# First mixer: normalising the window attention's probabilities in the product that turns them

## The chip, the cores and the metric

The kernel runs on one core of a Trainium2 chip. The metric is the device time of one execution in microseconds; the time before is the median of three runs. The engines are called as in the profile: PE (matrix products), PEld (the loading of PE's stationary operand, beside PE), DVE (elementwise work and reductions), ACT (activation functions and copies), POOL (small elementwise work, some DMAs) and SP (most DMAs).

## The reference, cut to what matters

The program is an encoder trunk of two layers. Layer 0 has windowed attention as its token mixer, layer 1 a gated linear recurrence; each mixer also has four cross-attention heads into 256 memory tokens, and each layer ends with a convolutional feed-forward part. There are 1024 tokens of width 1024, all in fp32. The change lies in the windowed attention of layer 0, with 16 query heads and 4 key heads of width 64:

```python
def window_gqa_sink(q, k, v, sink):
    ...
    s = jnp.einsum('bnqhgd,bnkhd->bnhgqk', qb, kb, preferred_element_type=F32) * (d ** -0.5)
    ...
    s = jnp.where(valid[None, :, None, None], s, -jnp.inf)
    sk = sink.astype(F32).reshape(hkv, grp)[None, None, :, :, None, None]
    m = jnp.maximum(jnp.max(s, axis=-1, keepdims=True), sk)
    p = jnp.exp(s - m)
    p = p / (jnp.sum(p, axis=-1, keepdims=True) + jnp.exp(sk - m))
    o = jnp.einsum('bnhgqk,bnkhd->bnqhgd', p.astype(v.dtype), vb)
```

A block of 128 queries sees its own 128 keys and the 128 on each side. The row sum by which `p` is divided includes the sink's term.

## The kernel before, in words

The attention is in `window()`. It works on four head groups `g` (one key head and four query heads each), and for each of them on eight blocks `n` of 128 queries: 32 blocks of four heads. `proj(g)` makes a group's queries, keys and values out of the normed input (tile `pj`, three products for each pair of operands, L84 to L86, where each operand is split into a high and a low part), applies the rotation and turns the result by transposes (tile `ptq`, L320). `attend(g, ...)` does the blocks.

In a block, for each of the four heads `j`: two products give the scores in `ps` (L366, L367; two banks), and one DVE instruction adds the mask and writes the negated scores to `sm` with their minimum in `nm` (L369). ACT then makes the exponentials in place and their sums `su` (L373); the sink stands as one more column behind the scores, put there by POOL (L362). `rd` is the reciprocal of the four sums (L375). Then the rows of `sm` are scaled by `rd`, head 0 on ACT (L378), heads 1 to 3 on DVE (L380). For each of the two or three key blocks `c`, four PE transposes (L385, one for each head, `sm` as the stationary operand and the identity `ident` as the moving one) put the turned probabilities into a bank `pt` (two banks), and ACT, or DVE for `c == 1`, copies it to `pT` (L387). The products with the values `v` into `po` follow at L395, in plain fp32, with high priority. There are 22 key blocks in eight query blocks, so 88 in all and 352 transposes.

The memory cross-attention (`cross_unit`) runs between the blocks with banks of the same names. The kernel already has a product with a diagonal, at its start (L1509 to L1513): the rows' scale `rsm` times the identity is `dg`, and `ones` times `dg` spreads it over the partitions, in fp32.

What order the instructions have on an engine is settled when the kernel is built: a scheduler runs a timeline model of the whole program and issues by priorities, so a change of one step moves others around it. Within an engine instructions run in that order. While a group's blocks run, the projection of the next group is spread between them; beside the last group stands the output projection (`pb`, class `Out`).

Of the kernel before, what the change touches and what calls it, by code (L numbers as in the profile page):

```python
# [8 lines left out]
F32 = mybir.dt.float32  # L9
# [3 lines left out]
AF = mybir.ActivationFunctionType  # L13
# [5 lines left out]
P = 128  # L19
# [30 lines left out]
def build(tc, A, out):  # L50
    nc = tc.nc
    act, dve, pool, pe = nc.scalar, nc.vector, nc.gpsimd, nc.tensor
# [13 lines left out]
    ident = cp.tile([P, P], F32, name="ident")  # L66
# [21 lines left out]
    def split(h, l, src):  # L88
        return act.copy(h, src), dve.tensor_tensor(l, src, h.bitcast(F32), op=ALU.subtract)  # L89
# [103 lines left out]
    def cross_head(l, h, wp, behind=None):  # L193
        kvh = wp.tile([P, 2, 256], F32R, tag="kvh", bufs=1, name="kvh")
        kvl = wp.tile([P, 2, 256], F32R, tag="kvl", bufs=1, name="kvl")
        raw = kvl.bitcast(F32)
        nc.sync.dma_start(raw, kvd[l][h])
        with tc.issue_after(behind.ins) if behind else nullcontext():
            act.copy(kvh, raw)
        dve.tensor_tensor(kvl, raw, kvh.bitcast(F32), op=ALU.subtract)  # L200
        return *wunit(A["wxq"][l, h]), kvh, kvl
# [47 lines left out]
    def window():  # L249
        ea = tc.alloc_tile_pool(name="attn0", bufs=1, reuse_waits="tile")  # L250
        ap_ = tc.alloc_tile_pool(name="attn", bufs=2, side="right", reuse_waits="tile")
# [25 lines left out]
        def proj(g):  # L277
# [56 lines left out]
            if g == 0:  # L334
                rqs = [token(t) for t in range(5)]
                turn(0, rqs[:4])
                attend(0, kept, range(3))
                turn(1, rqs[4:] + [token(t) for t in range(5, NT)])
            else:
                for b in range(2):  # L340
                    turn(b, [token(t) for t in range(4 * b, 4 * b + 4)])
# [6 lines left out]
        def attend(g, qkv, blocks=range(NT)):  # L348
            qs, kh, kl, v = qkv
            for b in range(2):  # L350
                for nn in range(4):
                    n = 4 * b + nn
                    if n not in blocks:
                        continue
                    if nn % 2 == 0 and g < 3:
                        pairs[0] = [ea.tile([P, 2, 256], F32R, tag=x, bufs=2, name=x) for x in ("oh", "ol")]
                    lo, hi = max(n - 1, 0), min(n + 2, NT)
                    w = (hi - lo) * P
                    mo = (lo - (n - 1)) * P
                    sm = ap_.tile([P, 4, 385], F32, tag="sm", bufs=3, name="sm")  # L360
                    st = {x: ap_.tile([P, 4], F32, tag=x, name=x) for x in ("nm", "su", "rd")}
                    pool.tensor_copy(sm[:, :, w:w + 1], sk[:, 4 * g:4 * g + 4].unsqueeze(2))  # L362
                    for j in range(4):
                        s = psp.tile([P, 384], F32, tag="ps", bufs=2, name="ps")
                        m = slice(nn * P, (nn + 1) * P)
                        pe.matmul(s[:, :w], qs[j][b][:, m], kh[:, lo * P:hi * P], start=True, stop=False)  # L366
                        pe.matmul(s[:, :w], qs[j][b][:, m], kl[:, lo * P:hi * P], start=False, stop=True)  # L367
                        hd = 4 * g + j
                        dve.tensor_tensor_reduce(out=sm[:, j, :w], in0=s[:, :w], in1=wmask[:, mo:mo + w],  # L369
                                                 scale=-0.125, scalar=sk[:, hd:hd + 1], op0=ALU.add, op1=ALU.min,  # L370
                                                 accum_out=st["nm"][:, j:j + 1])
                    for j in range(4):
                        marks[g, n] = act.activation(sm[:, j, :w + 1], sm[:, j, :w + 1], AF.Exp, bias=st["nm"][:, j:j + 1],  # L373
                                                     scale=-1.0, accum_out=st["su"][:, j:j + 1])
                    dve.reciprocal(st["rd"], st["su"])  # L375
                    for j in range(4):
                        if j < 1:
                            act.activation(sm[:, j, :w], sm[:, j, :w], AF.Copy, scale=st["rd"][:, j:j + 1])  # L378
                        else:
                            dve.tensor_scalar_mul(sm[:, j, :w], sm[:, j, :w], st["rd"][:, j:j + 1])  # L380
                    pTs = []
                    for c in range(hi - lo):
                        tp = psp.tile([P, 4, P], F32, tag="pt", bufs=2, name="pt")
                        for j in range(4):
                            pe.transpose(tp[:, j, :], sm[:, j, c * P:(c + 1) * P], ident)  # L385
                        pT = ap_.tile([P, 4, P], F32, tag="pT", bufs=3, name="pT")
                        (dve.tensor_copy if c == 1 else act.copy)(pT, tp)  # L387
                        pTs.append(pT)
                    po = psp.tile([P, 2, P], F32, tag="po", bufs=1, name="po")
                    with tc.high_priority(AHEAD):  # L390
                        mm = None
                        for c in reversed(range(hi - lo)):
                            for i in range(2):
                                with tc.issue_after(mm.ins) if mm else nullcontext():
                                    mm = pe.matmul(po[64 * i:64 * i + 64], v[:, lo + c, :], pTs[c][:, i::2, :],  # L395
                                                   start=c == hi - lo - 1, stop=c == 0, tile_position=(0, 64 * i))
                    if g == 3:
                        split(uh[:, 6:8, n * P:(n + 1) * P], ul[:, 6:8, n * P:(n + 1) * P], po)
                        continue
                    split(*(x[:, :, (nn % 2) * P:(nn % 2 + 1) * P] for x in pairs[0]), po)  # L400
                    if nn % 2 == 1:
                        ts_ = slice((n - 1) * P, (n + 1) * P)
                        for i, x in enumerate(pairs[0]):
                            nc.sync.dma_start(oS[2 * g:2 * g + 2, :, i, ts_].rearrange("a p t -> p a t"), x.bitcast(F32))
                if 4 * b + 3 not in blocks:
                    continue
                for _ in range(XU[g][b]):
                    xh_, xb_ = units.pop(0)
                    if xb_ == 0:
                        xhead[0] = cross_head(0, xh_, ea, None if xh_ else marks[0, 3])  # L410
                    cross_unit(0, xh_, xb_, xhead[0], ap_, tags, ea, pair)
# [3 lines left out]
        for g in range(3):  # L415
            attend(g, cur, range(0 if g else 3, NT))
            cur = proj(g + 1)
        ea.release()
        tables.release()
        attend(3, cur)  # L420
        wo0.open()
        y0 = wo0.w1.tile([P, NT, 512], F32, bufs=1, name="y0")
# [1207 lines left out]
```

## Time and profile before

| what | value |
| --- | --- |
| median of 3 runs | 2615.66 us (2615.55 to 2616.15) |
| profiled execution, its own time | 2614.47 us |
| span of its instructions | 2612.7 us, 39059 instructions |
| PE busy / its weight loads | 2587.9 us (99%) / 2172.6 us (83%) |
| DVE / ACT / POOL busy | 1762.1 us / 1332.8 us / 453.5 us |
| TensorE clock granted in the span | 1.00 |
| transposes of L385 | first start 98.8 us, last 460.1 us |

A group's row has the line of the program, the engine, the operation, the tiles (written<-read), the shape, how many, then the busy time in us with the mean of one in ns, and the idle time of the engine ahead of them with what ended it. In a timeline row the first two numbers are start and length in us; a merged row (x8) runs from the first start to the last end. A matmul's record overlaps the next one's, so PE's busy share alone doesn't say how full it is.

### The profile page before, as it was taken

Reading aid. Unit: us, or ns where it says so; the run is one execution under the profiler, and the core shown is the slowest. Engines: PE = TensorE matmul, PEld = TensorE weight load, DVE = VectorE, ACT = ScalarE, POOL = GpSimd, SP = SyncE. Lnnn points to the kernel's source line nnn. Section 1 sums busy time; section 2 is a strip of 40 time slices with the busy share of each in tenths; the row PEclk is TensorE's granted clock in tenths of the full one; section 3 lists DMA queues with packets and bytes.
Section 4 is the critical chain, followed back from the end, with each engine's and each line's share of the span. In section 5 each row is a group of like instructions: output and inputs, shape, how many; then the busy total and the mean of one; then the engine's idle time right before and its main releaser. Section 6 shows DMA issues by size and latency. Waiting matters only on the chain.

```text
span 2612.7 us, 39059 instructions
## 1 busy us (share of the span) xinstructions
PE 2587.9 (99%) x14596; PEld 2172.6 (83%) x14596; DVE 1762.1 (67%) x2839; ACT 1332.8 (51%) x2395; POOL 453.5 (17%) x520
## 2 busy tenths in 40 slices
PE   8999999999999999999999999999999999999998
PEld 8988887888888888887888888888888888888887
DVE  6677775577565664488698696987768655656447
ACT  6566665444444454454555454555534444444453
POOL 0431110211111100032133131221211111110013
PEclk9999999999999999999999999999999999999999
DMA  9782342467877757673236341213337777875666
GB/s 357 257 204 67 101 147 60 141 179 201 209 209 201 190 160 262 194 266 109 80 130 167 81 113 41 61 38 109 130 113 189 212 202 195 206 204 175 211 192 237
DMA packets 203918, 431.17 MB, mean 165 GB/s; under 512 B 20048, under 2 KB 64464, under 8 KB 198096
## 3 DMA queue, kind: packets, MB, share of 16 engines
q1 hardware_dynamic: 169744, 329.30, 38.7%
q0 software_dynamic: 24544, 90.19, 16.5%
q10 hardware_dynamic: 9440, 9.19, 1.1%
q8 instruction: 114, 1.87, 0.3%
q14 instruction: 76, 0.62, 0.1%
HBM read 333.18 MB, written 119.54 MB: 173 GB/s over the span
## 4 chain that ended last, share of the span: by engine, by line
PE 91%; DVE 5%; DMA 2%; ACT 1%; issue 0%; POOL 0%; SPq 0%; ACTq 0%; DVEq 0%; POOLq 0%
PE X L580 31%; PE V L580 11%; PE pj L84 7%; PE pj L85 7%; PE pj L86 7%; PE Y L580 5%; PE pb L84 4%; PE pb L85 4%; PE pb L86 4%; PE po L395 2%; PE pt L385 1%; PE po L1344 1%; PE pa L1265 1%; PE pu L1320 1%; PE ps L366 1%; PE pt L122 1%
## 5 line engine op out<-in xcount | busy, mean ns | idle before, releaser
L89 DVE TENSOR_TENSOR wl<-st,wh 128x1024 fp32r<-128x1024 f32 (+1 forms) x238 | 261.6, 1108 | 315.3 <-ACT wh L89 282.7
L89 ACT CAST wh<-st 128x1024 fp32r<-128x1024 f32 (+1 forms) x238 | 221.6, 937 | 268.0 <-PE X L580 172.2
L580 PE MATMUL X<-wh,wl 128*128 128x512 f32 x528 | 204.8, 389 | 0.0
L580 PE MATMUL X<-wl,wh 128*128 128x512 f32 x528 | 204.8, 389 | 0.0
L84 PE MATMUL pj<-uh,wh 128*128 128x512 f32 x512 | 202.3, 396 | 2.4 <-DVE s L1187 1.4
L86 PE MATMUL pj<-uh,wl 128*128 128x512 f32 x512 | 202.1, 395 | 0.0
L85 PE MATMUL pj<-ul,wh 128*128 128x512 f32 x512 | 201.5, 394 | 0.1
L580 PE MATMUL X<-wh 128*128 128x512 f32 x528 | 198.0, 390 | 0.1
L84 PE MATMUL pj<-wh,uh 128*128 128x384 f32 (+1 forms) x512 | 189.1, 370 | 2.0 <-DVE gs L1168 1.4
L85 PE MATMUL pj<-wl,uh 128*128 128x384 f32 (+1 forms) x512 | 187.1, 365 | 0.0
L86 PE MATMUL pj<-wh,ul 128*128 128x384 f32 (+1 forms) x512 | 186.9, 365 | 0.0
L80 DVE TENSOR_TENSOR wl<-st,wh 128x1024 fp32r<-128x1024 f32 (+1 forms) x91 | 118.3, 1306 | 29.3 <-ACT wh L79 28.1
L580 PE MATMUL V<-uh,wh 128*128 128x512 f32 x336 | 130.7, 389 | 0.0
L580 PE MATMUL V<-ul,wh 128*128 128x512 f32 x336 | 130.7, 389 | 0.0
L580 PE MATMUL V<-uh,wl 128*128 128x512 f32 x336 | 130.7, 389 | 0.0
L580 PEld LDWEIGHTS X<-wh 128*128 128x128 f32 x528 | 99.1, 188 | 21.1 <-issue 0.5
L79 ACT CAST wh<-st 128x1024 fp32r<-128x1024 f32 (+1 forms) x97 | 97.5, 1014 | 37.0 <-PE pj L85 23.9
L580 PEld LDWEIGHTS X<-wl,wh 128*128 128x128 f32 x528 | 99.1, 188 | 20.7 <-DVE wl L89 0.2
L580 PEld LDWEIGHTS X<-wh,wl 128*128 128x128 f32 x528 | 99.1, 188 | 20.4
L84 PEld LDWEIGHTS pj<-uh,wh 128*128 128x128 f32 x512 | 96.3, 188 | 21.9 <-DVE q L1182 1.4
L85 PEld LDWEIGHTS pj<-ul,wh 128*128 128x128 f32 x512 | 96.3, 188 | 19.2 <-DVE ul L89 0.4
L86 PEld LDWEIGHTS pj<-uh,wl 128*128 128x128 f32 x512 | 96.3, 188 | 18.9 <-issue 0.4
(412 smaller groups left out, 6986.7 us busy)
## 6 DMA issues: line engine op xcount, KB each, us to landing
st<-hid SPq DMA_DIRECT2D x154, 256.0 KB, 3.1
st<-in_ffw_dram SPq DMA_DIRECT2D x108, 256.0 KB, 3.3
w2s<-in_ffw_dram POOLq DMA_DIRECT2D x24, 1024.0 KB, 8.4
st<-in_ffw_dram SPq DMA_DIRECT2D x46, 512.0 KB, 4.3
hid<-tt SPq DMA_DIRECT2D x88, 256.0 KB, 4.8
st<-w2s SPq DMA_DIRECT2D x88, 256.0 KB, 3.3
sx<-in_ffw_dram SPq DMA_DIRECT2D x84, 256.0 KB, 3.9
sy<-in_ffw_dram SPq DMA_DIRECT2D x42, 512.0 KB, 6.4
```

The lines of the kernel that those rows point to most:

```text
L79: act.copy(h[:, :n], raw)
L80: (eng or dve).tensor_tensor(l[:, :n], raw, h[:, :n].bitcast(F32), op=ALU.subtract)
L84: pe.matmul(o, ah, bh, start=first, stop=False)
L85: pe.matmul(o, ah, bl, start=False, stop=False)
L86: return pe.matmul(o, al, bh, start=False, stop=last)
L89: return act.copy(h, src), dve.tensor_tensor(l, src, h.bitcast(F32), op=ALU.subtract)
L122: across = pe.transpose(ps[:, k, :], u[:, (4 * b + k) * P:(4 * b + k + 1) * P], ident)
L366: pe.matmul(s[:, :w], qs[j][b][:, m], kh[:, lo * P:hi * P], start=True, stop=False)
L385: pe.transpose(tp[:, j, :], sm[:, j, c * P:(c + 1) * P], ident)
L395: mm = pe.matmul(po[64 * i:64 * i + 64], v[:, lo + c, :], pTs[c][:, i::2, :], start=c == hi - lo - 1, stop=c == 0, tile_position=(0, 64 * i))
L580: last = pe.matmul(o, x, y, start=new, stop=e, skip_group_check=not first)
L1265: return pe.matmul(pa[i:i + 32, c, j:j + n], x[:, c * P + i:c * P + i + 32], y[:, c * P + j:c * P + j + n], start=True, stop=True, tile_po ...
```

## The change

The scaling at L378 and L380 goes. Instead DVE multiplies the identity by each head's `rd` (a diagonal of 128 x 128 for each head, in a new tile `dg` with two buffers), and the transpose by the identity becomes a plain fp32 product with that diagonal: out[k, q] = sum over r of sm[r, k] * dg[r, q], which is the turned and scaled block. ACT's part of the scaling has no successor.

```diff
                     dve.reciprocal(st["rd"], st["su"])
+                    dg = ap_.tile([P, 4, P], F32, tag="dg", bufs=2, name="dg")
                     for j in range(4):
-                        if j < 1:
-                            act.activation(sm[:, j, :w], sm[:, j, :w], AF.Copy, scale=st["rd"][:, j:j + 1])
-                        else:
-                            dve.tensor_scalar_mul(sm[:, j, :w], sm[:, j, :w], st["rd"][:, j:j + 1])
+                        dve.tensor_scalar_mul(dg[:, j, :], ident, st["rd"][:, j:j + 1])
                     pTs = []
                     for c in range(hi - lo):
                         tp = psp.tile([P, 4, P], F32, tag="pt", bufs=2, name="pt")
                         for j in range(4):
-                            pe.transpose(tp[:, j, :], sm[:, j, c * P:(c + 1) * P], ident)
+                            pe.matmul(tp[:, j, :], sm[:, j, c * P:(c + 1) * P], dg[:, j, :], start=True, stop=True)
```

In the changed kernel the lines behind this place have numbers lower by two: the products stand at L383, the copies at L385, `v*pT` at L393.

The scheduler lays the attention's instructions out anew. The first place is PE's order in the first block of the first group. Before:

```order
L84 MATMUL pj<-uh,wh 128x512
L385 MATMUL pt<-ident,sm 128x128 x2
L366 MATMUL ps<-kh,qs 128x384
L385 MATMUL pt<-ident,sm 128x128 x6
L367 MATMUL ps<-kl,qs 128x384
L85 MATMUL pj<-ul,wh 128x512
```

and now:

```order
L84 MATMUL pj<-uh,wh 128x512
L366 MATMUL ps<-kh,qs 128x384
L367 MATMUL ps<-kl,qs 128x384
L85 MATMUL pj<-ul,wh 128x512
L383 MATMUL pt<-dg,sm 128x128 x8
L366 MATMUL ps<-kh,qs 128x384
```

The block's eight products stand in one row, behind a head's scores and one projection product that stood within or behind the transposes.

The second place is PE's order at the start of the last head group, where no projection product stands between (`ptq` are the turned queries and keys, `po` the products with the values). Before:

```order
L320 MATMUL ptq<-ident,rq 128x128 x4
L366 MATMUL ps<-kh,qs 128x384
L367 MATMUL ps<-kl,qs 128x384
L385 MATMUL pt<-ident,sm 128x128 x8
L366 MATMUL ps<-kh,qs 128x384
L367 MATMUL ps<-kl,qs 128x384
L366 MATMUL ps<-kh,qs 128x384
L367 MATMUL ps<-kl,qs 128x384
L395 MATMUL po<-pT,v 64x256 x4
```

Now, from the third of six heads whose scores stand in a row:

```order
L366 MATMUL ps<-kh,qs 128x384
L367 MATMUL ps<-kl,qs 128x384
L366 MATMUL ps<-kh,qs 128x384
L367 MATMUL ps<-kl,qs 128x384
L366 MATMUL ps<-kh,qs 128x384
L367 MATMUL ps<-kl,qs 128x384
L366 MATMUL ps<-kh,qs 128x384
L367 MATMUL ps<-kl,qs 128x384
L383 MATMUL pt<-dg,sm 128x128 x8
L320 MATMUL ptq<-ident,rq 128x128 x4
```

The scores of six heads now come ahead of the block's products with the diagonal, where one to two heads stood between the other products.

The third place is DVE's order in the first block (`L369 ISA` is the masked minimum; each has a second instruction that reads out its result). Before:

```order
L380 TENSOR_SCALAR sm<-sm,rd 128x256 x3
L300 TENSOR_TENSOR t_1203<-pj,sin 128x320
L80 TENSOR_TENSOR wl<-st,wh 128x768
L369 ISA sm,nm<-ps,wmask,sk 128x384
L369 ISA nm 128x1
L387 COPY pT<-pt 128x512
```

and now:

```order
L378 TENSOR_SCALAR dg<-ident,rd 128x128 x4
L300 TENSOR_TENSOR t_1206<-pj,sin 128x320
L80 TENSOR_TENSOR wl<-st,wh 128x768
L369 ISA sm,nm<-ps,wmask,sk 128x384
L369 ISA nm 128x1
L369 ISA sm,nm<-ps,wmask,sk 128x384
L369 ISA nm 128x1
L385 COPY pT<-pt 128x512
```

Four diagonals stand where the three scalings stood, and the copy of the turned bank comes one head's minimum later. Behind the last block, in the output projection, PE's order is again what it was, from its 2330th row on.

## The prediction

> **What bounds the kernel now.** I read the page first, for the engine that sets the time.
>
> ```profile
> PE 2587.9 (99%) x14596; PEld 2172.6 (83%) x14596; DVE 1762.1 (67%) x2839; ACT 1332.8 (51%) x2395; POOL 453.5 (17%) x520
> ...
> PE 91%; DVE 5%; DMA 2%; ACT 1%; issue 0%; POOL 0%; SPq 0%; ACTq 0%; DVEq 0%; POOLq 0%
> ```
>
> PE is busy all the time, and 91% of the chain that ends last is PE's; the next engine, DVE, is busy for two thirds. But a busy PE need not be a full one: a matmul's record lasts longer than the time after which the next one may start. So I looked next at the timeline, for the distance from one start to the next, which is the price of an instruction on PE. These are, in order of time, the two products with a diagonal that the kernel already has at its start, six transposes of the changed line, eight transposes of a later norm, and four records of a plain fp32 product in the second mixer with what follows them (columns: start and length of the group in us, engine, line, out<-in, shape, count).
>
> ```profile
> 19.22 0.61 PE L1513 MATMUL pbc<-dg,ones 128*128 128x128 f32 x4
> ...
> 99.20 0.82 PE L385 MATMUL pt<-ident,sm 128*128 128x128 f32 x6
> ...
> 505.30 1.03 PE L122 MATMUL pt<-ident,nu 128*128 128x128 f32 x8
> ...
> 1313.46 0.61 PE L1344 MATMUL po<-S,qin 128*128 128x128 f32 x4
> 1313.91 0.39 PE L1344 MATMUL po<-v,As 128*128 128x128 f32 x2
> ```
>
> A merged row runs from the first start to the last end, and one record is 0.275 us long (the mean in the groups below). Eight transposes: (1.03 - 0.275) / 7 = 0.108 us from start to start; six: (0.82 - 0.275) / 5 = 0.109. I take **0.109 us for a transpose**. Four records of L1344: (0.61 - 0.275) / 3 = 0.112 us, and the starts agree, since 1313.46 to 1313.91 is 0.45 for four. L1513: 0.112 again. For the `v*pT` products there is a row of the chain of waits, which gives a record 1.45 / 12 = 0.121 us:
>
> ```profile
> 213.74 1.45 PE po L395 x12
> ```
>
> Is the attention stretch, where the change is, really full of such starts? I counted one window of it by the groups of instructions, kept apart by shape.
>
> ```profile
> L86 PE MATMUL pj<-wh,ul 128*128 128x384 f32 x38 | 12.8, 338 | 0.0
> L84 PE MATMUL pj<-wh,uh 128*128 128x384 f32 x37 | 12.8, 345 | 0.0
> L85 PE MATMUL pj<-wl,uh 128*128 128x384 f32 x37 | 12.5, 338 | 0.0
> L385 PE MATMUL pt<-ident,sm 128*128 128x128 f32 x52 | 7.6, 275 | 0.0
> L395 PE MATMUL po<-pT,v 128*64 128x256 f32 x60 | 7.6, 388 | 0.1
> L366 PE MATMUL ps<-kh,qs 128*128 128x384 f32 x18 | 6.7, 374 | 0.0
> L367 PE MATMUL ps<-kl,qs 128*128 128x384 f32 x18 | 6.1, 337 | 0.0
> ```
>
> This is 200 to 240 us. The 148 records of 384 columns at 0.174 us (the first two starts in the dense stretch below are 0.17 apart; 0.174 is the median of all such distances) are 25.8, 52 transposes at 0.109 are 5.7, 60 records of L395 at 0.121 are 7.3; with 4 transposes and 2 short score products not shown, some 0.7, that is 39.5 of 40 us. So PE has under 2% to spare here: **what is added to PE's own work in this stretch is added to the time**, and what is taken from ACT and DVE is not.
>
> **The change part by part.** The groups of the touched lines in the window 60 to 480 us:
>
> ```profile
> L385 PE MATMUL pt<-ident,sm 128*128 128x128 f32 x352 | 50.5, 275 | 0.6 <-ACT sm L378 0.6
> ...
> L380 DVE TENSOR_SCALAR sm<-sm,rd 128x384 f32<-128x384 f32 (+1 forms) x96 | 33.4, 406 | 0.8
> ...
> L378 ACT ACTIVATE sm<-sm,rd 128x384 f32<-128x384 f32 (+1 forms) x32 | 18.9, 590 | 3.4 <-DVE rd L375 3.3
> ```
>
> *PE.* The 352 transposes have one record each and become 352 products of an fp32 tile of 128 x 128 with an fp32 diagonal. What such a product is made of, the answer on the tile `dg` at the kernel's start tells:
>
> ```profile
> L1513 PE MATMUL pbc<-dg,ones x4: 273/274/275, 19.2 to 19.6; 128*128 128x128 f32 x4
> L1512 DVE TENSOR_SCALAR dg<-ident,rsm x2: 280/284/288, 16.7 to 16.9; 128x128 f32<-128x128 f32 x2
> ```
>
> There the program has two products (the loop over t at L1511 runs twice) and the trace four records, so a product is two passes. At 0.112 us each that is 0.224 per product against 0.109 per transpose: **+0.115 us x 352 = +40.5 us**, on PE and with nothing on PE to hide it. The ends of this term are 0.114 and 0.117 per product by the rounding of the rows, 40.1 and 41.2 us. Which operand is held in the array does not change: `sm` was loaded before and is now.
>
> [...]
>
> *ACT.* It loses 18.9 us of scaling. *DVE* loses 33.4 us and gets 128 rows of `dg` (four in each of 32 blocks) of 128 x 128, at 0.284 by L1512: 36.4 us, so +3.0. Both lie beside PE's matmuls, and I cost them at nothing; without that cover DVE's 3.0 us would be its price, and ACT's 18.9 us its gain. The way of one block stays as long: from `rd` to the last scaled head three times 0.406 us on DVE, now four times 0.284; 1.22 against 1.14 us.
>
> *Waits that can go.* PE's own waits in 60 to 500 us, the four longest of six rows:
>
> ```profile
> PE po L395 <- ACT pT L387: 0.9, 2, 0.7
> PE pt L385 <- ACT sm L378: 0.6, 1, 0.6
> PE po L395 <- DVE pT L387: 0.6, 1, 0.6
> PE pb L84 <- ACT y L492: 0.6, 1, 0.6
> ```
>
> These are 2.7 us in five waits, 3.4 with the two rows left out. A wait shows only beyond the end of the record before it, so each hides up to 0.17 us more (a 384-column record is 0.34 long, and the next may start after 0.17): 3.4 + 7 x 0.16 = 4.5 us is the most that can come back. One of them is of the removed step; the place is the start of the last head group, where there is little projection work between the score products:
>
> ```profile
> 385.06 0.34 PE L366 MATMUL ps<-kh,qs 128*128 128x384 f32 x1
> 385.23 0.34 PE L367 MATMUL ps<-kl,qs 128*128 128x384 f32 x1
> 386.15 1.08 PE L395 MATMUL po<-pT,v 128*64 128x256 f32 x8 [0.58 <-DVE pT L387]
> ...
> 389.49 0.34 PE L367 MATMUL ps<-kl,qs 128*128 128x384 f32 x1
> 390.42 1.09 PE L385 MATMUL pt<-ident,sm 128*128 128x128 f32 x8 [0.59 <-ACT sm L378]
> ...
> 391.89 0.34 PE L367 MATMUL ps<-kl,qs 128*128 128x384 f32 x1
> 392.78 0.50 PE L84 MATMUL pb<-wh,uh 128*128 128x512 f32 x1 [0.56 <-ACT y L492]
> ```
>
> From start to start, less 0.174 each, 0.75 + 0.76 + 0.72 = 2.2 us are lost here. The middle one waits for ACT's scaled head and goes: **-0.8**. DVE's diagonals are then what is late next.
>
> *Waits that can come.* At the same place the new order has six heads' score products in a row with nothing between (second place in the section on the change). There are two score banks, and DVE empties one in 0.612 us (the median, in the answer on the tile `sm`):
>
> ```profile
> L369 DVE CUSTOM_DVE_ANT_0 sm<-ps,wmask,sk x128: 474/612/621, 86.0 to 446.5; 128x384 f32<-128x384 f32 x96, 128x256 f32<-128x256 f32 x32
> ```
>
> PE needs 2 x 0.174 = 0.35 for a head, so from the third of the six on it waits 0.26 for each: 4 x 0.26 = **+1.1 us**. Behind the waiting score product stand, in order, the products with the diagonal, then the transposes of queries. Bounds: nothing, if DVE is ahead; and if three more stretches of the new order (one per head group) lose as much as this one did, 3 x 2.2 = 6.6 us more.
>
> Sum, on the profiled execution's 2614.47 us (span 2612.7): + 40.5 - 0.8 + 1.1 = 2655.3. The median of the three runs is 1.2 us above that execution, so **2656.5 us**.
>
> **The rivals.**
>
> *A transpose costs as much as its record is long, and the products are cheaper (faster).* The place is PE at L385, the price 0.275 us for each of 352 transposes against 0.224 now: 352 x 0.051 = -18.0 us, 2597.7 us. It decides if eight transposes in a row take more than 1.8 us. For it speaks only the mean of 275 ns; against it the eight in 1.03 us. [...]
>
> *PE has hidden room.* The products fill gaps that the page calls busy. 0.5 us in 40 were not accounted for above; over the 410 us of attention that is 5, with the dense stretch's 2.2 some 7. Even if all of it took up passes, 2649 us. To come out not slower, 40 us would be needed.
>
> [...]
>
> *The product is done as a transpose is, in one pass.* Then the change does not do what it says: 352 x (0.112 - 0.109) = +1.1 us, 2616.8. Against it, L1513 again, whose moving operand is a diagonal too.
>
> *Waits of a new kind in every block.* If each of the 32 blocks lost one wait like those in the dense stretch, 0.75 us, it would be 24 us more, 2680. For it: PE's order is rearranged from the first block to the output projection behind the last, and DVE has 3 us more to do. Against it: a bank of products now takes PE 0.90 us where four transposes took 0.44, so those who empty it (ACT's copies) have twice the time.
>
> **How the numbers follow.** The forecast has 0.89. Its range: below, 2615.7 + 40.1 - 4.5 = 2651; above, 2615.7 + 41.2 + 1.1 + 6.6 = 2664.6. I set 2650 to 2665; the room of the second rival reaches to its lower end. The others: faster 0.01, hidden room that takes more than 7 us 0.03, four passes 0.02, one pass 0.01, waits in every block 0.04. A measurement of this kernel tells a difference from none at about 0.2%, 5 us. So faster by more 0.01, within it 0.02 (the one pass, and a hundredth for room that I don't see), slower 0.97.
>
> **What would show it.** The line of the products should have 704 records in place of 352, with eight of them (four products) from start to start in 0.9 us. L378's group is gone from ACT, `dg` stands on DVE with 128 rows of about 0.28 us. From 500 us on, everything stands as before and some 41 us later. I am wrong in the price if the records are 352 or 1408, wrong in the cover if the span grows by over 50 us with 704 records at 0.112, and wrong on the room if it grows by under 34.

## The result, and the profile after

The changed kernel takes **2659.5 us** (median of four runs, 2658.56 to 2662.13) beside 2615.61 us for the one before on the same chip: ratio 1.0169, interval 1.0157 to 1.0181, so 43.9 us slower. The forecast was 2656.5 us in a range of 2650 to 2665. The profiled execution is the highest of the four, 2662.13 us with a span of 2660.4, which is 47.7 us more than the span before. So readings of this trace hold for 47.7 us, and the medians for 43.9. One execution each of e4, e6 and e12 below ran for 3235 to 6689 us and is left out of their medians, ranges and ratios.

The page of the kernel after, first busy time by engine, then the share of each engine in the chain that ended last:

```profile
PE 2631.3 (99%) x14948; PEld 2217.7 (83%) x14948; DVE 1760.2 (66%) x2871; ACT 1318.0 (50%) x2363; POOL 447.6 (17%) x520
...
PE 86%; DVE 7%; DMA 3%; ACT 1%; issue 1%; POOL 1%; SPq 0%; ACTq 0%; DVEq 0%; POOLq 0%
```

PE has 352 records more, and ACT and DVE are a little less busy than before. PE has lost five points of the chain, two of them to DVE: somewhere PE stands and waits. Both parts show in closer views. First the groups of the touched lines in the window 60 to 540 us:

```profile
L383 PE MATMUL pt<-dg,sm 128*128 128x128 f32 x704 | 92.3, 278 | 0.0
...
L378 DVE TENSOR_SCALAR dg<-ident,rd 128x128 f32<-128x128 f32 x128 | 31.1, 305 | 0.9
```

704 records stand where 352 stood, none of them after a wait. The distance from start to start is in PE's timeline, in the first block:

```profile
100.08 1.95 PE L383 MATMUL pt<-dg,sm 128*128 128x128 f32 x16
```

Eight products are 16 records, and (1.95 - 0.275) / 15 = 0.112 us. The price of one product is 0.224 us, as forecast.

The waits are in PE's own list for 60 to 540 us (waiting tile and line, what for, us in all, times, longest):

```profile
PE pb L84 <- ACT v L304: 2.5, 1, 2.5
PE ps L366 <- ACT kh L89: 1.3, 1, 1.3
PE ps L366 <- DVE nm L369: 1.1, 2, 0.8
```

The two longest are neighbours. This is PE's timeline at that place, the start of the last head group:

```profile
401.77 0.60 PE L320 MATMUL ptq<-ident,rq 128*128 128x128 f32 x4
403.68 0.50 PE L366 MATMUL ps<-kh,qs 128*128 128x256 f32 x2 [1.31 <-ACT kh L89]
406.68 0.80 PE L84 MATMUL pb<-wh,uh 128*128 128x512 f32 x1 [2.50 <-ACT v L304]
407.27 0.63 PE L85 MATMUL pb<-wl,uh 128*128 128x512 f32 x1
407.69 0.63 PE L86 MATMUL pb<-wh,ul 128*128 128x512 f32 x1
...
412.73 0.40 PE L86 MATMUL pb<-wh,ul 128*128 128x512 f32 x1
```

From start to start, less 0.109 for each transpose and 0.120 for each product of 256 columns, PE loses 1.91 - 0.44 = 1.5 us and then 3.00 - 0.24 = 2.8 us. After that the records are 0.63 us long where 0.39 is usual, and their starts are 0.42 to 0.43 us apart where they are 0.227 apart elsewhere: 14 starts take 412.73 - 406.68 = 6.05 us and would take 3.18, another **2.9 us**. The view by windows has the reason (PE, PEld, DVE, ACT and POOL busy with their counts, then PE's granted clock, the DMA share and GB/s):

```profile
400.00:406.00 6.00, 2.87 (x18) 2.39 (x16) 5.97 (x6) 3.60 (x4) 2.15 (x2) 0.98 0.81 227
406.00:413.00 7.00, 6.33 (x16) 4.98 (x17) 1.76 (x4) 0.63 (x2) 2.29 (x4) 0.53 0.61 240
413.00:426.00 13.00, 11.86 (x69) 9.51 (x68) 8.25 (x30) 6.70 (x20) 0.14 (x1) 1.00 0.01 1
```

The granted clock falls to a half during the second wait (0.89 over 405 to 406 us, 0.50 over 406 to 407), and in the 6 us of the first window DVE is busy for 5.97 and PE for 2.87. What PE waits for is in the timelines of ACT and of DVE:

```profile
398.84 4.17 ACT L79 CAST wh<-st 128x1024 fp32r<-128x1024 f32 x4 [0.69 <-PE pj L86]
403.04 0.59 ACT L89 CAST kh<-ptq 128x512 fp32r<-128x512 f32 x1
```

```profile
399.93 5.42 DVE L80 TENSOR_TENSOR wl<-st,wh 128x1024 fp32r<-128x1024 f32 x4 [1.05 <-ACT wh L79]
405.39 0.49 DVE L299 TENSOR_TENSOR t<-pj,cos 128x320 f32<-128x320 f32 x1
405.79 0.48 DVE L300 TENSOR_TENSOR t<-pj,sin 128x320 f32<-128x320 f32 x1
```

Four weight tiles of the output projection are cast on ACT and split on DVE; behind them in the queues stand the keys `kh` and the last rotations of this group's projection. Only after these rotations does ACT get to `v` (L304), the instruction that the profile names as the one PE waits for: the output projection (`pb`) is written into the banks of `pj`, which the rotations and `v` still read. PE has nothing to put in: in its order no projection product stands between the group's last one and the output projection.

### The profile page after: what moved, and what is told of

Same layout as the page of the kernel before. It is cut to its first block, busy times and chain, and to the rows that moved or that the text cites. A ratio compares the mean times of both kernels' runs of the same rounds, so it can differ in the third digit from the quotient of the medians.

```text
span 2660.4 us, 39787 instructions
## 1 busy us (share of the span) xinstructions
PE 2631.3 (99%) x14948; PEld 2217.7 (83%) x14948; DVE 1760.2 (66%) x2871; ACT 1318.0 (50%) x2363; POOL 447.6 (17%) x520
## 4 chain that ended last, share of the span: by engine, by line
PE 86%; DVE 7%; DMA 3%; ACT 1%; issue 1%; POOL 1%; SPq 0%; ACTq 0%; DVEq 0%; POOLq 0%
PE X L578 27%; PE V L578 11%; PE pj L84 7%; PE pj L85 7%; PE pj L86 7%; PE Y L578 4%; PE pb L84 4%; PE pb L85 4%; PE pb L86 4%; PE pt L383 3%; PE po L393 2%; PE po L1342 1%; DVE wl L89 1%; PE pa L1263 1%; PE pu L1318 1%
## 5 line engine op out<-in xcount | busy, mean ns | idle before, releaser
L373 ACT ACTIVATE sm<-sm,nm 128x385 f32<-128x385 f32 (+1 forms) x128 | 75.1, 587 | 75.2 <-DVE nm L369 71.3
```

## Experiments

Two questions are open: is the price that of the second pass, with the softmax side worth nothing; and does the hole at 402 to 413 us (PE's two long waits and the half clock with them) belong to the diagonals or to the order the scheduler happened to make? To count, I took the starts of PE and subtracted from each distance the price of the instruction by its width (0.227 us for 512 columns, 0.174 for 384, 0.120 for 256, 0.109 for a transpose, 0.112 for a pass of the product, 0.121 for `v*pT`). A pass, here as in the prediction, is one record of a product. What is left over is time in which PE is late. The table has this for one profiled execution of each kernel, worked out by me from the trace; the third row is the first three head groups, the fourth from 6 us ahead of the first `pb` product to 30 us behind it.

| us | before | after | e1 | e9 | e2 | e6 |
| --- | --- | --- | --- | --- | --- | --- |
| span | 2612.7 | 2660.4 | 2652.1 | 2654.4 | 2622.5 | 2621.8 |
| sum of prices | 2579.4 | 2619.9 | 2619.9 | 2619.9 | 2579.4 | 2579.4 |
| late, three groups | 8.6 | 6.8 | 6.5 | 6.7 | 15.7 | 12.6 |
| late, start of last group | 3.3 | 9.8 | 3.0 | 2.6 | 3.6 | 7.2 |
| late, elsewhere | 6.8 | 8.8 | 8.0 | 10.0 | 8.6 | 7.8 |

Before and after differ by 40.5 in prices (704 x 0.112 less 352 x 0.109, so put in and not found), -1.8 in the three groups, +6.5 at the start of the last and +2.0 elsewhere: 47.2 of the 47.7 us.

### The price of the product

**e1_ident** is the kernel before with the product in place of the transpose, the identity as its moving operand and the scaling kept:

```diff
-                            pe.transpose(tp[:, j, :], sm[:, j, c * P:(c + 1) * P], ident)
+                            pe.matmul(tp[:, j, :], sm[:, j, c * P:(c + 1) * P], ident, start=True, stop=True)
```

> The scaling stays on ACT and DVE as before, and the turned block is a plain fp32 product with the identity: only PE's part of the change is made. Theory (two passes for one, on a PE that is full): 352 products of 0.224 us for 352 transposes of 0.109, so 2615.6 + 40.5 = 2656 us, within 4 us for waits of its own order, and 704 records on the products' line. Rival (a part of the 44 us is the diagonals on DVE, or what the shorter way through ACT moves): below 2645 us.

Measured: 2653.79 us (2653.04 to 2655.21) beside 2615.84, ratio 1.0144 (1.0127 to 1.0161), +38.0. Its group, 60 to 560 us:

```profile
L385 PE MATMUL pt<-ident,sm 128*128 128x128 f32 x704 | 92.2, 278 | 0.0
```

The same 704 records, without any diagonal: the product alone brings nearly all of the loss. The start of the last group loses 3.0 us, as little as before.

**e8_products_twice** issues every product of the changed kernel twice:

```diff
-                            pe.matmul(tp[:, j, :], sm[:, j, c * P:(c + 1) * P], dg[:, j, :], start=True, stop=True)
+                            for _ in range(2):
+                                pe.matmul(tp[:, j, :], sm[:, j, c * P:(c + 1) * P], dg[:, j, :], start=True, stop=True)
```

> The changed kernel with each product with the diagonal done twice into the same place, 1408 records. Theory: 352 more products at 0.224 us are 78.9 us more than the changed kernel without its hole, 2656 + 79 = 2735 us, 2731 to 2740 with its own waits. Rival (PE takes the products partly into its gaps, and the 40 us are partly something else): less than 2725 us.

Measured: 2740.32 us (two runs) beside 2616.5 on its chip, ratio 1.0472 (1.0453 to 1.0491), +123.8. That is 79.9 us more than the change itself brought, 0.227 us for each of 352 products against 0.224 by the starts. The time lies 0.3 us above the range that was expected, and the 0.227 holds only as far as the hole in the changed kernel and the one in e8, below, cost about the same.

Its group, 60 to 600 us:

```profile
L384 PE MATMUL pt<-dg,sm 128*128 128x128 f32 x1408 | 171.9, 276 | 0.0
```

Here the order was laid out anew once more. The hole at the last group is gone, and another has come at 220 us, with a half clock of its own behind a wait for DVE (granted clock 0.57 over 224 to 228 us):

```profile
223.81 0.44 PE L366 MATMUL ps<-kh,qs 128*128 128x384 f32 x1 [3.15 <-DVE nm L369]
...
224.31 0.63 PE L85 MATMUL pj<-ul,wh 128*128 128x512 f32 x1
```

**e4_one_pass** makes both operands fp32r, the format of the projections, so that a product is one pass. **e7_one_pass_look** is the same kernel again, for its profile.

```diff
-                    sm = ap_.tile([P, 4, 385], F32, tag="sm", bufs=3, name="sm")
+                    sm = ap_.tile([P, 4, 385], F32R, tag="sm", bufs=3, name="sm")
...
-                    dg = ap_.tile([P, 4, P], F32, tag="dg", bufs=2, name="dg")
+                    dg = ap_.tile([P, 4, P], F32R, tag="dg", bufs=2, name="dg")
```

> The changed kernel with sm and the diagonal in the reduced fp32 format that the projections use: the products keep their count, shape and diagonals, and are one record each; scores, exponentials and reciprocals are rounded to that format. Theory (the price is the second pass): 352 records of 0.11 us, 2612 to 2621 us. Rival (the price is the longer load of a plain stationary tile, 0.19 against 0.14 us, and not the number of passes): above 2630 us.

> The kernel with one-pass products again, for its profile. Theory: 352 records on the products' line, four of them 0.11 us from start to start though the stationary tile's load has the length of a plain one (0.19 us), and PE's work elsewhere as before.

Measured: 2617.68 and 2618.19 us beside 2615.84 and 2616.5, ratios 1.0006 (0.9997 to 1.0016) and 1.0005 (0.9995 to 1.0015): some 2 us more than before, which can't be told from no change. The groups of e7, 60 to 560 us:

```profile
L383 PE MATMUL pt<-dg,sm 128*128 128x128 f32 x352 | 50.2, 272 | 0.1
L383 PEld LDWEIGHTS pt<-dg,sm 128*128 128x128 f32 x352 | 47.7, 190 | 8.0 <-issue 5.4 <-DVE kl L89 0.4 <-DVE nm L369 0.4
```

and its PE timeline in the first block:

```profile
100.08 1.00 PE L383 MATMUL pt<-dg,sm 128*128 128x128 f32 x8
```

One record for each product, (1.00 - 0.275) / 7 = 0.104 us from start to start. The weight load before each is 190 ns by its own row, longer than the whole distance, and yet the products follow one another at that pace. So a weight load with a longer record (a transpose's at L385 in the kernel before is 141 ns) costs nothing here; the second pass is what costs. With the diagonals kept and the scaling gone, e7 is still no faster than before: by the count of the table its three groups lose 14.1 us where before loses 8.6, in an order of its own.

**e2_no_scale** is the kernel before without the scaling. It is the most that relief of ACT and DVE could bring.

```diff
-                    for j in range(4):
-                        if j < 1:
-                            act.activation(sm[:, j, :w], sm[:, j, :w], AF.Copy, scale=st["rd"][:, j:j + 1])
-                        else:
-                            dve.tensor_scalar_mul(sm[:, j, :w], sm[:, j, :w], st["rd"][:, j:j + 1])
```

> The kernel before without any scaling of the probabilities (the division by the row sums is left out): ACT loses 18.9 us and DVE 33.4 us of work, PE's work stays. Theory (both lie beside a full PE): 2611 to 2617 us, no more than the 4.5 us of waits can come back. Rival (ACT and DVE hold PE up, so that relief counts and the diagonals cost): 2605 us or less.

Measured: 2623.98 us (2622.93 to 2625.02), ratio 1.0032 (1.0021 to 1.0043), **8.1 us slower** with work taken out. No theory had that. Its waits on PE, 60 to 560 us, the first three rows:

```profile
PE ps L366 <- DVE nm L369: 1.9, 3, 1.3
PE pt L380 <- ACT sm L373: 1.5, 1, 1.5
PE po L390 <- DVE ol L89: 1.2, 1, 1.2
```

and one of them in PE's timeline:

```profile
331.29 0.27 PE L380 MATMUL pt<-ident,sm 128*128 128x128 f32 x1
333.03 0.33 PE L380 MATMUL pt<-ident,sm 128*128 128x128 f32 x1 [1.47 <-ACT sm L373]
```

With a step fewer in its model, the scheduler placed some transposes at points where ACT's exponentials are not yet done, and PE stands before them; the waits for DVE are longer too. That the shorter model is the reason is argued, not shown. The prices are the same 2579.4 us as before; the three groups lose 15.7 us in place of 8.6. What was learnt is not what was asked: the relief gave nothing in the order that came out, and the order alone can cost 8 us.

### The hole at the start of the last group

**e3_late_weights** starts the output projection's weights only after the last group's last rotation:

```diff
-        wo0.open()
+        with tc.issue_after(roped[0].ins):
+            wo0.open()
```

> The changed kernel, with DVE's splitting of the output projection's weights put behind the last rotation of queries and keys. Theory (some 3 us of the 44 are one hole at the start of the last head group: PE waits 1.5 and 2.7 us while DVE splits four weight tiles, and then runs at half clock for 6 us): the waits are shorter, the clock stays at 1.00, and the time is 2653 to 2657 us. Rival (the 3 us are spread over the attention's blocks): within 1 us of the changed kernel's 2659.5, with or without the hole.

Measured: 2661.92 us (2661.16 to 2662.36), ratio 1.0174 (1.0159 to 1.019): no gain, and a miss for both theories. Its waits on PE, 60 to 540 us, and its clock:

```profile
PE ps L366 <- ACT kh L89: 1.3, 1, 1.3
...
PE pb L84 <- ACT v L304: 1.0, 2, 0.6
```

```profile
408.00:415.00 7.00, 6.27 (x18) 4.98 (x19) 6.49 (x14) 1.68 (x5) 0.68 (x1) 0.58 0.73 225
```

The 2.5 us wait is broken into smaller ones, and the clock falls all the same. The weights are in the way, but later weights leave PE as empty as before: by the count of the table e3 loses 9.9 us at this place, the kernel after 9.8. The missing piece is other work for PE.

**e5_after_moved** and **e6_before_moved** move one unit of the memory cross-attention from the first to the second half of the third group's blocks, in the changed kernel and in the one before:

```diff
-XU = [(0, 2), (0, 2), (2, 2), (0, 0)]
+XU = [(0, 2), (0, 2), (1, 3), (0, 0)]
```

> The changed kernel with one cross-attention unit moved from the middle to the end of the third head group (XU[2] = (1, 3) for (2, 2)), so that PE has projection and cross-attention work left when the last group begins. Theory (43.9 = 40.5 for the passes and 3.4 for one hole with half clock behind it): no stretch of half clock at the start of the last group, and 2653 to 2657 us. Rival (the 3.4 us belong to the diagonals and are found in any order): 2658 us or more, with full clock.

> The kernel before with the same move of one cross-attention unit. The theory prices the change at the second passes whatever the order, so between this kernel and the changed one with the move stand 40.5 us, within 2. By itself the move should cost or gain little, 2611 to 2618 us: before has no hole at that place, only 2.2 us of short waits. Rival: the difference between the two moved kernels is again 43 us or more.

Measured: e5 2660.26 us (2658.26 to 2661.5), ratio 1.0164 (1.015 to 1.0178); e6 2624.02 us (2622.41 to 2624.62), ratio 1.0027 (1.0016 to 1.0038). Both missed: the hole stayed in the one and came up in the other. The difference of the two is 36.2 us, under the 40.5 within 2 that was expected: e6 loses 12.6 us in the three groups and e5 7.5 by the same count, and among e6's waits there is 1.0 us for ACT's scaling, the step that the change removes. PE's timeline of e5 and then of e6 at this place shows one wait of the same length:

```profile
402.35 0.40 PE L366 MATMUL ps<-kh,qs 128*128 128x256 f32 x2
404.89 0.50 PE L84 MATMUL pb<-wh,uh 128*128 128x512 f32 x1 [2.14 <-ACT v L304]
```

```profile
376.70 0.40 PE L366 MATMUL ps<-kh,qs 128*128 128x256 f32 x2
379.23 0.51 PE L84 MATMUL pb<-wh,uh 128*128 128x512 f32 x1 [2.13 <-ACT v L304]
```

So **the hole is possible with transposes and with scaling**: it belongs to an order, not to the diagonals. The clock is what differs, by the windows of e5 and then of e6:

```profile
406.00:410.00 4.00, 4.00 (x14) 3.13 (x13) 2.66 (x4) 0.31 (x1) 1.91 (x3) 0.57 0.98 346
```

```profile
380.00:384.00 4.00, 4.00 (x21) 3.33 (x20) 3.83 (x8) 0.79 (x3) 1.65 (x2) 1.00 0.97 350
```

**e9** and **e10** leave the changed kernel's steps alone and give the last group's projection more priority, 200 or 450; **e11** and **e12** do the same to the kernel before.

```diff
-            cur = proj(g + 1)
+            with tc.high_priority(200) if g == 2 else nullcontext():
+                cur = proj(g + 1)
```

> The changed kernel with the last head group's projection 200 steps of priority earlier, so that cross-attention and projection products stand behind the transposes of its queries. Theory (the price of the passes is 40.5 us in any order, the rest is PE's waits and the half clock behind a long one): no wait of more than 1.2 us in the attention, full clock in it, 2650 to 2656 us. Rival (the 3.4 us beyond the passes belong to the diagonals): 2658 us or more, spread over the blocks.

> The same with 450 steps. Theory: again the passes and the waits of this order alone, 2649 to 2657 us, with full clock if no wait of PE passes 2 us. Rival: as for 200 steps, 2658 us or more.

> The kernel before with 200 steps. Theory: the changed kernel with the same step stands 36 to 40.5 us above it, the second passes less what they take up of PE's waits for the softmax (3 to 5 us in the pair with the moved unit); by itself 2611 to 2619 us. Rival (PE's gaps take nothing up): 40.5 us or more.

> The kernel before with 450 steps. Theory: 36 to 40.5 us below the changed kernel with 450 steps; by itself 2610 to 2619 us. If it is below 2613, the order alone is worth more than the waits that the profile of before shows at one place. Rival: a distance of 40.5 us or more.

| kernel | median, us | ratio to before, interval |
| --- | --- | --- |
| e9, after with 200 | 2654.01 (2651.67 to 2656.24) | 1.0142 (1.0127 to 1.0158) |
| e10, after with 450 | 2655.57 (2654.5 to 2657.0) | 1.0152 (1.0138 to 1.0166) |
| e11, before with 200 | 2615.52 (2613.92 to 2618.95) | 0.9999 (0.999 to 1.0008) |
| e12, before with 450 | 2620.79 (2618.39 to 2623.51) | 1.002 (1.001 to 1.0029) |

In e9's timeline cross-attention and projection products stand among the last group's first score products. Its window, and the first two rows of its waits (60 to 540 us):

```profile
400.00:420.00 20.00, 19.28 (x108) 15.55 (x106) 15.01 (x38) 11.51 (x29) 4.31 (x5) 1.00 0.46 159
```

```profile
PE pj L84 <- ACT v L304: 0.9, 2, 0.5
PE ptq L320 <- DVE qs L331: 0.5, 1, 0.5
```

The hole is gone, the clock stays full in the attention, and the changed kernel is 2659.5 - 2654.0 = **5.5 us** faster for it (its own steps unchanged). Where the attention has no such hole on either side, e9 less e11, the change costs **38.5 us**. e9's profile is not clean to its end: in the second mixer PE is busy for 3.96 of 6 us, and behind that the granted clock is 0.66 over 5 us, a half for some 3.4 of them. This is part of the 10.0 us "elsewhere" in the table.

```profile
1535.00:1541.00 6.00, 3.96 (x82) 3.09 (x80) 3.54 (x5) 1.73 (x3) 2.27 (x3) 1.00 1.03 228
1541.00:1546.00 5.00, 5.00 (x17) 3.98 (x16) 3.81 (x6) 3.65 (x7) 0.00 (x0) 0.66 0.96 249
```

e10 less e12 is 34.8, under the 36 to 40.5 expected, and e12 by itself lies above its 2610 to 2619, because it has a poor order of its own: a new wait, with half clock behind it (0.72 over 386 to 392 us).

```profile
386.84 1.94 PE L239 MATMUL pt<-ident,xp 128*128 128x128 f32 x8 [1.45 <-DVE xp L234]
```

No version here beats the kernel before.

## Why the prediction was right

- **Two passes of 0.112 us for one transpose of 0.109, +40.5 us.** Right in kind and size: 704 records at 0.112 in the trace, +38.0 with the product alone (e1), 0.227 us for a product more (e8), +2 us with one pass (e4, e7). The rival with a product in one pass falls with it. So do four passes, which have 0.02 among the chances: no run shows a plain fp32 product of four records, the traces have two for each, 704 for 352 and in e8 1408 for 704. What a record is made of, no run shows either. In the `v*pT` row at 142.35 below, two records start 7 ns apart and the next two 216 ns later by the starts in the trace, where fp32r records of 256 columns follow every 120 ns.
- **ACT and DVE at nothing.** Right. In sign the term of DVE was off: +3.0 us forecast, 31.1 - 33.4 = -2.3 by the groups' rows, since four diagonals in a row overlap (128 of 0.305 us would be 39.0, not 31.1) and I had multiplied their single lengths. It made no difference to the time. That the relief is worth nothing was not shown cleanly by e2, whose order became worse; e1, which keeps the scaling, and e9, which has none, differ by 0.2 us without a hole in the attention, and that is the better evidence. In e6's order 1.0 us of PE's waits was for the scaling, so the term is nothing in these orders and not in every one.
- **Waits that can go, -0.8, at most -4.5.** The forecast gain was too small, within its bound. The wait of L378 is gone, and the slower products take up others: the three groups lose 6.4 to 6.8 us in e1, e9, e10 and after, where before loses 8.6 and e11 9.0. In the kernel before a wait of this sort is

```profile
142.35 1.51 PE L395 MATMUL po<-pT,v 128*64 128x256 f32 x12 [0.68 <-ACT pT L387]
```

and PE's list of the kernel after has no row `po` behind ACT's `pT`. A bank takes PE longer to fill (0.90 us for eight records at 0.112, where four transposes took 0.44), and those who empty it are late less often. This is the forecast's rival of hidden room, at 2 us rather than the 40 it would have needed; 40.5 less some 2 would be the 38.0 of e1 and the 38.5 of e9 less e11. This is not shown: the spans of the profiled executions differ by 39.4 and 40.8 there, since what the three groups gain is in part lost elsewhere. I read it from the waits; no run tried it alone.
- **Waits that can come, +1.1.** The place was right, and the size near. PE's timeline of the kernel after in the six heads whose scores stand in a row:

```profile
420.13 0.34 PE L367 MATMUL ps<-kl,qs 128*128 128x384 f32 x1
420.79 0.45 PE L366 MATMUL ps<-kh,qs 128*128 128x384 f32 x1 [0.32 <-DVE nm L369]
...
421.61 0.34 PE L367 MATMUL ps<-kl,qs 128*128 128x384 f32 x1
422.76 0.44 PE L366 MATMUL ps<-kh,qs 128*128 128x384 f32 x1 [0.82 <-DVE nm L369]
```

  From start to start, less 0.174, that is 0.49 + 0.98 = 1.5 us, in two waits instead of four of 0.26, because DVE also works on the turned queries between the minima (L329, 0.68 us at 421.30).
- **The step that missed something.** The same term left out the hole just ahead of that place: 1.5 + 2.8 us of waits and 2.9 us at half clock. Its upper bound, three more dense stretches for 6.6 us, covered the amount, not the mechanism. What made the hole is four weight splits ahead of the last rotations on DVE, and no projection product left on PE. I looked at what stood behind the score products and not at what PE had ahead of them, and held the clock at 1.00 throughout.
- **+1.2 us from the profiled execution to the median.** Wrong in sign for the kernel after, whose profiled execution lies 2.6 us above its median. On its own scale the sum was 2655.3 against 2662.1, short by 6.8 us, about the hole; on the medians it was short by 3.0. The closer agreement of the medians is luck.
- **From 500 us on as before, some 41 us later.** Nearly. The first product of the feed-forward part, before and then after (shortest, median and longest in ns, then the first and the last start in us):

```profile
L580 PE MATMUL V<-uh,wh x336: 389/389/389, 575.4 to 2392.0; 128*128 128x512 f32 x168
```

```profile
L578 PE MATMUL V<-uh,wh x336: 389/389/389, 621.3 to 2439.3; 128*128 128x512 f32 x168
```

  It starts 45.9 us later and the last one 47.3: the loss is complete where the attention ends, apart from 1.4 us.

What stays open is why the scheduler's model chose that order for the changed kernel. e3 and e5 show that neither the weights' time nor one unit's place alone decides it, and e9 and e10 only that more priority for the projection avoids it.

## What to carry to other kernels

Count an engine that is full by the distance between starts, and count what a product is made of by its records: here two existing products of the same kind in the old trace gave the price of 352 new ones to within 3 us. Moving work from idle engines to the full one was a loss here, even though it saved them some 20 us. And when a change makes a scheduler lay the order out anew, look for places where the full engine runs out of work, ahead of the part you watch as well as behind it; compare old and new in two orders each before you charge a loss to the change itself.

## What the runs showed of the hardware

PE's granted clock was a half for some microseconds in or just behind a wait of PE. By the windows that was 6.8 us in the kernel after (0.89 over 405 to 406 us, 0.50 over each of the next six, 0.70 over 412 to 413), about as much in e3 (0.94 over 400 to 408 us, 0.58 over 408 to 415), and about 3.4 us in e5 (0.57 over 406 to 410), e8 (0.57 over 224 to 228), e9 (0.66 over 1541 to 1546) and e12 (0.72 over 386 to 392). PE was late there by 2.3 us in e5, 3.3 in e8, some 2.0 in e9, and 1.5 and 2.8 in the kernel after; in e12 it was the 1.45 of the row at 386.84 behind several shorter ones, and in e3 no wait in the attention is longer than 1.3. The same 2.3 us in e6 brought no drop (1.00 over 376 to 388 us). So the length of a wait alone doesn't tell whether the clock falls, and the 2 us in e10's expectation are not shown as a limit. What decides it stays open.

At half clock transposes slow down too. In e12's row at 386.84 (0.72 over 386 to 392 us) eight of them take 1.94 us from first start to last end, where the eight of a norm quoted in the prediction take 1.03 at a granted clock of 1.00.
